# A hybrid decoder block on one core: output projection by operand, first queries ahead, norm weight per partition, table loads moved, last projection reordered, query copies on ScalarE

## The chip, the cores and the metric

The kernel runs on one core of a Trainium2 chip. A core has TensorE (matrix products, in the profile PE, its weight loads PEld), VectorE (DVE), ScalarE (ACT), GpSimd (POOL, here mostly a queue that issues transfers) and SyncE (SP, a second such queue). SBUF is the working memory of 128 partitions; PSUM holds the sums of the products. The metric is the device time of one execution in microseconds, as the median of several runs.

## The reference

One decoder block of width 1024 over 2048 positions. What is computed, cut to its frame:

```python
mod = (silu(c) @ w_ada + b_ada)                       # six vectors: sh1, sc1, g1, sh2, sc2, g2
h = rms_norm(x, norm1_g) * (1 + sc1) + sh1
gq, gk, gv, gr, glr, aq, ak, av = split(h @ w_in)     # one projection for both head groups
log_a = log_sigmoid(glr @ gla_w_gate + gla_b_gate) / 16
y_gla = gla_group(gq, gk, gv, log_a, gr, gla_norm_g)  # 4 heads of gated linear attention,
                                                      # per head rms_norm * gla_norm_g, times silu(gr)
y_att = dilated_attention_group(rms_norm(aq, q_norm_g), rms_norm(ak, k_norm_g), av)
                                                      # 8 heads, windows (128,1), (512,4), (2048,16)
x = x + g1 * (concat(y_gla, y_att) @ w_out)
h = rms_norm(x, norm2_g) * (1 + sc2) + sh2
u = causal_depthwise_conv(h @ w_up, conv_w, conv_b)   # width 3
u_gate, u_val = split(u)
x = x + g2 * ((silu(u_gate) * u_val) @ w_down)        # inner width 2816
```

All data are float32.

## The kernel before

**Tiling.** Positions are cut into four chunks of 512 (`NCH`, `T`), channels into blocks of 128. An activation tile is 128 channels by 512 positions. The large products run in three passes: an operand is split into a rounded high part and the rest, and `mm3` (L311) issues, for each block of 128 input channels, high x high (L317), high x low (L318) and low x high (L319) into one PSUM tile. Weights come through `wslot` (L243): a load into `wraw` on the POOL queue (L246), a cast to the high part on ScalarE (L251) and a difference on VectorE (L252). `plan` (L261) lists all weight blocks in the order in which the products use them, and `weights` (L300) keeps three of them ahead; `wraw` has two buffers, the parts four each.

**Stages.** Each chunk `c` goes through four:

- `proj` (L499) makes the input projection. Its operations are `q0` to `q7` (`qk`, L515: four query and four key blocks of 128 channels, that is two heads each, squares, block sums on TensorE at L526 and L527, Ln and Exp at L528 and L529, three Newton operations on VectorE at L424 to L426, the scaled result at L532, permuted copies at L536 for queries or L539 and L542 for keys), `g0` to `g3` (`glaqk`, queries and keys of the linear attention, leaving through ScalarE at L553), `W0` and `W1` (`wide`, L559: values and output gate, positions on the partitions, four PSUM tiles at once) and `V0`, `V1` (`av`, values of the attention and the low-rank gate input). The order is `ORDER0` for chunk 0 and `ORDER` for the others. `W1` holds the output gate: Tanh (L579), a copy (L580), a product (L581) and a product with `gla_norm_g`, which lies broadcast over the partitions as `gB` (L583).
- `mix` (L1067) runs `gla` (L671) for two halves of the chunk, then `attn` (L828) for four pairs of heads. `gla` prepares decayed keys and queries at several scales (L732 to L736), makes scores (L712), outputs and state (L784 to L794), takes the root of the mean square with Sqrt (L799), multiplies by the gate (L805), transposes (L811) and stores `y` through two buffers named "stage" (L814). `attn_first` (L818) loads keys and queries of the next pair of heads, the queries also into a "stage" buffer; the first pair's is called when `attn` starts (L831).
- `outproj` (L1075) loads the eight tiles of `y`, splits them (L1088, L1089), and multiplies by `w_out`: for each of eight output blocks all eight operands in turn, and the residual at L1095. The last tile, `ylast`, comes from SBUF. Then the second norm follows, and work put off to here (`self.tail`): `W1` of chunk 3 in chunk 0, the last down-projection of the chunk before in the others.
- `ffn` (L1103) makes the up-projection with convolution and gate in six groups and the down-projection (`down`, L1145).

**Order.** `run` (L1171) interleaves these as generators: `beside` and `along` (L114, L128) advance one for so many steps of another. The products of the projections of chunks 1 to 3 run beside `mix(0)`; the last five operations of the projection of chunk 3, then `outproj(0)` and `ffn(0)`, beside `mix(1)`; and so on, `outproj(3)` and `ffn(3)` alone. Over this the framework plans each engine's order with a list scheduler that has a timing model (`TC`, L38), by the order of the program as priority; each engine then runs its list strictly in order, and so do the queues of SP and POOL.

**Buffers that matter here.** PSUM has eight banks: four "psg" tiles for the large products and four "psa" for the rest. "stage" has two buffers, "pt" five. `hhi`/`hlo` have ten buffers, `ghi`/`glo` five; `y0`/`y1` two each.

**Function tables.** ScalarE holds one set of function tables. One set has Exp and Tanh, one Sqrt, one Ln and Exp together. A function outside the present set is preceded by a load (ACT_TABLE_LOAD). The set with Ln and Exp is asked for by name at the start (L339) and in `gate` (L658).

Of the kernel before, what the change touches and what calls it, by code (L numbers as in the profile page):

```python
# [32 lines left out]

ORDER0 = "g0 g1 g2 g3 V0 q0 q1 W0 q2 q3 V1 q4 q5 q6 q7 W1".split()
ORDER = "W0 V0 q0 q1 q2 g0 q3 V1 q4 g1 q5 q6 g2 q7 g3 W1".split()

# [73 lines left out]

TABS = (KD, KD, 48, 1, 1, 132, 44, 4)

# [35 lines left out]
class K:  # L148
# [49 lines left out]
    def consts(self):  # L198
        nc, A = self.nc, self.A
        self.ct = self.const.tile(list(CONSTS.shape), F32, name="consts_sb")  # L200
        self.after(nc.sync.dma_start(self.ct, A["consts"]))
        n0 = len(self.loads)
        self.mk = self.cload("masks", MASKS.shape, U32)
        self.halo = self.const.tile([P, 44, 2], F32, name="halo")

        raw = self.at.tile([P, T], F32, name="graw", tag="pt", bufs=5)
        self.gw = self.const.tile([96, 256], F32R, name="gw")
        self.tie(nc.vector.memset(raw[0:96, 0:256], 0.0), self.lastmm)
        for r in (0, 32, 64):
            self.loads.append(nc.sync.dma_start(raw[r:r + 16, 0:256], A["gla_w_gate"]))  # L210
            if r < 64:
                self.loads.append(nc.sync.dma_start(raw[r + 16:r + 17, 0:256], A["gla_b_gate"]))
        nc.vector.tensor_copy(self.gw, raw[0:96, 0:256])
        nc.vector.tensor_tensor(self.gw[32:64], raw[32:64, 0:256], self.gw[32:64].bitcast(F32), op=ALU.subtract)
        self.gB = self.cload("gla_norm_g", (P, P))
        for ld in self.loads[n0:]:
            self.after(ld)
        self.blk = self.const.tile([P, P], F32R, name="blk")
        self.tri = self.const.tile([P, P], F32R, name="tri")
        sums = self.at.tile([P, T], F32, name="sums", tag="pt", bufs=5)  # L220
        self.after(nc.sync.dma_start(sums[:, 0:2 * P], A["sums"]))
        for i, t in enumerate((self.blk, self.tri)):
            self.tie(nc.vector.tensor_copy(t, sums[:, i * P:(i + 1) * P]), self.lastmm)
        self.st = self.const.tile([P, 4, P], F32, name="state")
        nc.vector.memset(self.st, 0.0)
        self.sb = []
        for i in range(2):
            t = self.const.tile([P, 4, P], F32, name=f"sbd{i}")
            nc.vector.memset(t, 0.0)
            self.sb.append(t)  # L230
# [30 lines left out]
    def plan(self):  # L261

        def proj(c):
            for o in ORDER if c else ORDER0:
                b = int(o[1])
# [26 lines left out]
        for c in range(NCH):  # L292
            yield from (("w_out", (b,), KD, P) for b in range(KD))
            if c:
                yield from down(5)
            else:
                yield from (("w_tokw", (1, j), 2, T) for j in range(4))
            yield from ffn(c)
# [24 lines left out]
    def ada_setup(self):  # L323
# [4 lines left out]
        o = np.cumsum((0,) + TABS)  # L328
        self.n1, self.n2, self.ba, self.qg, self.kg, cw, self.cb, qsc = (tab[:, o[i]:o[i + 1]] for i in range(len(TABS)))
        self.cw = cw.rearrange("p (a b) -> p a b", a=3)  # L330
        self.qgs = self.const.tile([P, 4], F32, name="qgs")
        self.kgs = self.const.tile([P, 1], F32, name="kgs")
        self.ones = self.const.tile([P, P], F32R, name="ones")
# [4 lines left out]
        tanh = nc.scalar.activation(th, self.cond, AF.Tanh, scale=0.5)  # L338
        pre = nc.scalar.preload_act_table_set("natural_log_exp_and_others")  # L339
        self.tc.add_manual_dep(pre.ins, tanh.ins.name, mybir.DependencyInfo(mybir.DependencyClass.Sync, mybir.DependencyReason.DATA))  # L340
        nc.vector.scalar_tensor_tensor(self.cond, th, 1.0, self.cond, op0=ALU.add, op1=ALU.mult)
        nc.vector.tensor_scalar(self.qgs, qsc, self.qg[:, 0:1], -0.5, op0=ALU.mult, op1=ALU.mult)
        nc.vector.tensor_scalar(self.kgs, self.kg, -0.5, None, op0=ALU.mult)
        self.mod = self.const.tile([P, 48], F32, name="mod")
        self.G1 = self.const.tile([P, KD], F32, name="G1")
# [41 lines left out]
    def ada_late(self):  # L387
# [5 lines left out]
        for n in range(len(parts) + 2):  # L393
# [15 lines left out]
            yield  # L409


    def load_x(self, c):
# [86 lines left out]
    def proj(self, c, hs, hook=None, done=()):  # L499
# [15 lines left out]
        def qk(b):  # L515
# [19 lines left out]
            if b < 4:  # L535
                nc.vector.tensor_copy(o4.rearrange("p (r m) -> p r m", r=4), o.rearrange("p (m r) -> p r m", r=4))  # L536
                self.dq.dma_start(D["q"][b], o4)
# [21 lines left out]
        def wide(b):  # L559
# [14 lines left out]
            for s in range(4):  # L574
                off = b and put_off
                st = stage("y0" if off else None)
                if b:
                    r = stage("y1" if off else None)
                    nc.scalar.activation(st, pss[s], AF.Tanh, scale=0.5)  # L579
                    nc.scalar.copy(r, pss[s])  # L580
                    nc.vector.scalar_tensor_tensor(st, st, 1.0, r, op0=ALU.add, op1=ALU.mult)  # L581
                    heads = lambda t: t.rearrange("p (a n) -> p a n", a=4)
                    nc.vector.scalar_tensor_tensor(heads(st), heads(st), 0.5, self.gB[:, None, :].to_broadcast([P, 4, P]), op0=ALU.mult, op1=ALU.mult)  # L583
                else:
                    nc.scalar.copy(st, pss[s])  # L585
# [46 lines left out]
        ops = dict(W=wide, V=av, g=glaqk, q=qk)  # L632
        order = ORDER if c else ORDER0
        if put_off:
# [4 lines left out]
    def gate(self, c, gl):  # L639
# [12 lines left out]
        for a in range(2):  # L652
            ps = self.pa()
            for s in range(2):
                mm = nc.tensor.matmul(ps[:, s * 256:(s + 1) * 256], glr[0:96, (2 * a + s) * P:(2 * a + s + 1) * P], self.gw, start=True, stop=True)
            if a == 0:

                self.tie(nc.scalar.preload_act_table_set("natural_log_exp_and_others"), mm)  # L658
            t = self.up.tile([P, T], F32, name="gt", tag="y1")
# [10 lines left out]

    def gla(self, c, a):  # L671
        nc, D = self.nc, self.D[c]
# [105 lines left out]
        for s in range(2):  # L778
# [19 lines left out]
            yield  # L798
        nc.scalar.activation(ss, ss, AF.Sqrt, bias=self.eps, scale=1.0 / P)  # L799
        nc.vector.reciprocal(ss, ss)  # L800
        ys = []
        for s in range(2):
            y = t2("pt", 5)
            for hd in range(4):
                nc.vector.scalar_tensor_tensor(y[:, hd * P:(hd + 1) * P], os[s][:, hd * P:(hd + 1) * P], ss[:, s, hd:hd + 1], rg[s][:, hd * P:(hd + 1) * P], op0=ALU.mult, op1=ALU.mult)  # L805
            ys.append(y)
        yield
        for s in range(2):
# [3 lines left out]
            st = t2("stage", 2)  # L812
            self.copy(st, ps)
            nc.sync.dma_start(D["y"][0:4].rearrange("h p n -> p h n")[:, :, (2 * a + s) * P:(2 * a + s + 1) * P], st.rearrange("p (h n) -> p h n", h=4))  # L814
# [3 lines left out]
    def attn_first(self, c, hp):  # L818
# [3 lines left out]
        for i in range(c + 1):  # L822
            nc.sync.dma_start(kt[:, i], D[i]["k"][hp])
        qf = self.at.tile([P, T], F32, name="qf", tag="stage", bufs=2)
        nc.sync.dma_start(qf, D[c]["q"][hp])
        return kt, qf

    def attn(self, c, hp, ready):  # L828
        nc, D = self.nc, self.D
        nk = 32 * (c + 1)  # L830
        kt, qf = ready.pop() if ready else self.attn_first(c, hp)  # L831
        qn = self.at.tile([P, T], F32, name="qn", tag="pt", bufs=5)
# [233 lines left out]

    def mix(self, c):  # L1067
        for a in range(2):
            yield from self.gla(c, a)
        ready = []  # L1070
        for hp in range(4):
# [3 lines left out]
    def outproj(self, c):  # L1075
        nc, A = self.nc, self.A
        hs = []
        for k in range(KD):
            if c or k > 5:
                hi, lo = (self.hp.tile([P, T], F32R, name=n) for n in ("hhi", "hlo"))  # L1080
            elif k == 5:
                hi, lo = (self.up.tile([P, T], F32R, name=n, tag=n) for n in ("y0", "y1"))
# [8 lines left out]
        x1 = self.load_x(c)  # L1091
        for cb in range(KD):
            ps = self.pg()
            self.mm3(ps, self.weights("w_out", cb), hs)
            nc.vector.scalar_tensor_tensor(x1[cb], ps, self.mod[:, 16 + cb:17 + cb], x1[cb], op0=ALU.mult, op1=ALU.add)  # L1095
            yield
# [210 lines left out]
def layout(x, c, w_ada, b_ada, norm1_g, w_in, gla_w_gate, gla_b_gate, gla_norm_g, q_norm_g, k_norm_g, w_out, norm2_g, w_up, conv_w, conv_b, w_down):  # L1307
# [3 lines left out]
    twice = lambda a: np.concatenate([a, a])[:, None]  # L1311
    tabs = np.concatenate([colv(norm1_g[0]), colv(norm2_g[0]), colv(b_ada[0]), twice(q_norm_g[0]), twice(k_norm_g[0]), conv_w[0].reshape(3, 44, P).transpose(2, 0, 1).reshape(P, 132), colv(conv_b[0]), scale_table()], 1).astype(np.float32)
    arrs = dict(
# [7 lines left out]
        w_ch=pack_blocks(np.concatenate([w[:, 0:512], w[:, 1552:2576]], 1), P),  # L1321
        gla_w_gate=gla_w_gate[0], gla_b_gate=gla_b_gate, gla_norm_g=np.broadcast_to(gla_norm_g.reshape(1, P), (P, P)),
        w_out=pack_blocks(w_out[0], P), w_up=pack_blocks(w_up[0], P), w_down=pack_down(w_down[0]),
    )
# [17 lines left out]
```

## Time and profile before

| | us |
|---|---|
| median of three runs (2571.28 to 2572.19) | 2571.36 |
| the profiled execution | 2572.54 |
| its span, first to last instruction | 2570.7 |
| TensorE busy | 2536.8 |
| VectorE busy | 1908.6 |
| ScalarE busy | 1270.1 |
| GpSimd busy | 446.9 |
| mean granted TensorE clock, share of full | 0.997 |

A group row of the profile reads: line, engine, operation, output <- inputs, output and input shapes, count, then busy time in us and the mean of one in ns, then the idle time of the engine just ahead and what ended it. A row of a timeline reads: start in us, duration, engine, line, operation, tiles, and in brackets the idle time before it with its releaser. A row of waits reads: who waited, on whom, us in total, how often, longest. A matmul's row in the timeline is longer than its share of the engine, since matmuls overlap; the distance between two starts is what one costs.

### The profile page before, as it was taken

The numbers are of one execution on the slowest core, as the hardware profiler recorded it, in microseconds if no ns is written. First come the engines' busy times: TensorE is split into PE (matmuls) and PEld (weight loads), VectorE is DVE, ScalarE is ACT, GpSimd is POOL, SyncE is SP. The second block draws the span as 40 slices with busy tenths as digits, with TensorE's granted clock in tenths as the row PEclk, the third lists the DMA queues.
The fourth block names the chain that finished last, engine by engine and source line by source line (L and its number), as shares of the span: only waits on it lengthen the run. The fifth ranks groups of instructions, "written<-read, shape, count | busy, mean of one in ns | idle before, by whom it ended". The sixth has DMA issues, their size and how long they took to land.

```text
span 2570.7 us, 49713 instructions
## 1 busy us (share of the span) xinstructions
PE 2536.8 (99%) x19458; PEld 2092.3 (81%) x19458; DVE 1908.6 (74%) x4135; ACT 1270.1 (49%) x2624; POOL 446.9 (17%) x814
## 2 busy tenths in 40 slices
PE   7999999999999999999999999999999999999999
PEld 4888788888788888888888888888888888888887
DVE  7678877767778677777977777778777776766665
ACT  5556756655554444454545444445445443433332
POOL 2333332322310000112100000310000003200001
PEclk9999999999999999999999999999999999999999
DMA  8775675665733344446434444743444536433332
GB/s 328 265 239 188 201 251 163 222 214 162 238 120 91 115 138 141 129 158 200 140 97 131 141 141 143 232 141 107 122 141 143 149 103 209 141 97 99 98 99 82
DMA packets 189727, 406.38 MB, mean 158 GB/s; under 512 B 48515, under 2 KB 89525, under 8 KB 188213
## 3 DMA queue, kind: packets, MB, share of 16 engines
q0 software_dynamic: 88096, 308.59, 36.9%
q1 hardware_dynamic: 101396, 94.60, 12.5%
q8 instruction: 154, 2.52, 0.4%
q14 instruction: 81, 0.66, 0.1%
HBM read 341.25 MB, written 61.87 MB: 157 GB/s over the span
## 4 chain that ended last, share of the span: by engine, by line
PE 93%; DVE 2%; DMA 2%; issue 1%; ACT 1%; POOL 0%; POOLq 0%; DVEq 0%; ACTq 0%
PE psg L317 27%; PE psg L318 27%; PE psg L319 27%; PE psa L907 2%; PE psa L879 2%; PE psa L1034 2%; PE psa L712 2%; PE psa L930 1%; PE psa L1028 1%; PE psa L785 0%; PE psa L784 0%; PE psa L459 0%; PE psa L789 0%; PE psg L1212 0%; DMA y<-stage 0%
## 5 line engine op out<-in xcount | busy, mean ns | idle before, releaser
L317 PE MATMUL psg<-hhi,whi 128*128 128x512 f32 x1968 | 773.0, 394 | 0.3 <-DVE x L1163 0.3
L318 PE MATMUL psg<-hlo,whi 128*128 128x512 f32 x1968 | 770.3, 392 | 0.0
L319 PE MATMUL psg<-hhi,wlo 128*128 128x512 f32 x1968 | 770.0, 391 | 0.0
L251 ACT CAST whi<-wraw 128x1024 fp32r<-128x1024 f32 (+1 forms) x388 | 407.0, 1049 | 455.6 <-PE psg L318 392.0
L252 DVE TENSOR_TENSOR wlo<-wraw,whi 128x1024 fp32r<-128x1024 f32 (+1 forms) x388 | 474.7, 1224 | 205.7 <-ACT whi L251 198.1
L317 PEld LDWEIGHTS psg<-hhi,whi 128*128 128x128 f32 x1968 | 369.9, 188 | 78.1 <-issue 0.6
L319 PEld LDWEIGHTS psg<-hhi,wlo 128*128 128x128 f32 x1968 | 369.9, 188 | 77.2 <-issue 0.3
L318 PEld LDWEIGHTS psg<-hlo,whi 128*128 128x128 f32 x1968 | 369.9, 188 | 75.9 <-issue 0.7
L317 PE MATMUL psg<-ghi,whi 128*128 128x512 f32 x744 | 296.9, 400 | 0.3 <-DVE x L1163 0.3
L318 PE MATMUL psg<-glo,whi 128*128 128x512 f32 x744 | 293.4, 394 | 1.6 <-DVE glo L1089 1.6
L319 PE MATMUL psg<-ghi,wlo 128*128 128x512 f32 x744 | 293.0, 394 | 0.0
L246 POOL DMA_DIRECT2D wraw<-in_w_up_dram x176 | 96.8, 550 | 975.8 <-DVE wlo L252 764.1
L1163 DVE SCALAR_TENSOR_TENSOR x<-psg,mod,x 128x512 f32<-128x512 f32 x192 | 143.1, 748 | 116.2 <-PE psg L319 115.8
L317 PE MATMUL psg<-whi,hhi 128*128 128x512 f32 (+2 forms) x512 | 173.8, 344 | 2.2 <-ACT stg L585 1.5
L318 PE MATMUL psg<-wlo,hhi 128*128 128x512 f32 (+2 forms) x512 | 174.4, 342 | 0.0
L319 PE MATMUL psg<-whi,hlo 128*128 128x512 f32 (+2 forms) x512 | 173.2, 341 | 0.0
L317 PEld LDWEIGHTS psg<-ghi,whi 128*128 128x128 f32 x744 | 140.5, 189 | 31.5 <-issue 0.9
L318 PEld LDWEIGHTS psg<-glo,whi 128*128 128x128 f32 x744 | 140.4, 189 | 30.7 <-DVE glo L1089 2.3
L319 PEld LDWEIGHTS psg<-ghi,wlo 128*128 128x128 f32 x744 | 140.3, 189 | 29.6 <-issue 0.2
L1118 ACT ACTIVATE y<-psg,tables_sb 128x512 f32<-128x512 f32 x176 | 135.8, 772 | 5.4 <-PE psg L319 4.8
L1119 DVE SCALAR_TENSOR_TENSOR y<-psg,tables_sb,y 128x511 f32<-128x511 f32 x176 | 130.8, 743 | 3.5 <-ACT y L1118 3.4
L1120 DVE SCALAR_TENSOR_TENSOR y<-psg,tables_sb,y 128x510 f32<-128x510 f32 x176 | 130.6, 743 | 0.5
(279 smaller groups left out, 3610.5 us busy)
## 6 DMA issues: line engine op xcount, KB each, us to landing
wraw<-in_w_up_dram POOLq DMA_DIRECT2D x176, 512.0 KB, 3.8
wraw<-in_w_down_dram POOLq DMA_DIRECT2D x88, 512.0 KB, 3.8
wraw<-in_w_ch_dram POOLq DMA_DIRECT2D x44, 512.0 KB, 4.5
wada<-in_w_ada_dram POOLq DMA_DIRECT2D x64, 256.0 KB, 4.8
wraw<-in_w_tokw_dram POOLq DMA_DIRECT2D x32, 512.0 KB, 4.6
wraw<-in_w_out_dram POOLq DMA_DIRECT2D x32, 512.0 KB, 4.5
sq<-in_xT_dram POOLq DMA_DIRECT2D x48, 256.0 KB, 5.0
x<-x POOLq DMA_DIRECT2D x48, 256.0 KB, 5.4
```

Of the source, the lines that this page charges most:

```text
L246: ld = self.dq.dma_start(raw[:, :n], src)
L251: nc.scalar.copy(hi[:, :n], raw[:, :n])
L252: nc.vector.tensor_tensor(lo[:, :n], raw[:, :n], hi[:, :n].bitcast(F32), op=ALU.subtract)
L317: nc.tensor.matmul(ps, wh, hh, start=first and k == 0, stop=False, skip_group_check=shared)
L318: nc.tensor.matmul(ps, wh, hl, start=False, stop=False, skip_group_check=shared)
L319: self.lastmm = nc.tensor.matmul(ps, wl, hh, start=False, stop=k == n - 1, skip_group_check=shared)
L712: nc.tensor.matmul(sp[j:j + w, o + n * w:o + (n + 1) * w], kh[R, k0:k0 + w], qh[R, q0:q0 + w], start=True, stop=True)
L879: nc.tensor.matmul(at(i, hh, o, n)[H[z]], q(H[hh], i, z), key(H[hh], i, k0, n), start=True, stop=True, skip_group_check=True)
L1118: nc.scalar.activation(y, ps, AF.Identity, bias=self.cb[:, b:b + 1], scale=self.cw[:, 2, b:b + 1])
L1119: nc.vector.scalar_tensor_tensor(y[:, 1:], ps[:, :T - 1], self.cw[:, 1, b:b + 1], y[:, 1:], op0=ALU.mult, op1=ALU.add)
L1120: nc.vector.scalar_tensor_tensor(y[:, 2:], ps[:, :T - 2], self.cw[:, 0, b:b + 1], y[:, 2:], op0=ALU.mult, op1=ALU.add)
L1163: nc.vector.scalar_tensor_tensor(x1, ps, self.mod[:, 40 + cb:41 + cb], x1, op0=ALU.mult, op1=ALU.add)
```

## The change

1. `outproj`: the first four output blocks are made together, in four PSUM tiles, operand by operand: four weight blocks `w_outk`, each of two operands by 512 output channels, and within each all four outputs. The last weight block is ordered by output. Then four residual additions, and the other four output blocks as before. In chunk 0 the operands' buffers are dealt out anew: the first two operands take `hhi`/`hlo`, the next five `ghi`/`glo`, the last one `y0`/`y1`.
2. `attn_first` for the first pair of heads is called in the second `gla`, ahead of its transposes and stores; the query tile takes a "pt" buffer in place of a "stage" one.
3. `gla_norm_g` becomes a column per partition, `gy`, halved once at the start; the product at L583 and the broadcast tile go, and the evictions of the transposed outputs multiply by `gy`.
4. The set with Ln and Exp is asked for behind the Tanh at the start (as before), behind the last Tanh of each `W1` but the put-off one, and behind the Sqrt of chunk 0; no longer in `gate`.
5. The projection of chunk 3 has its own order, `ORDER3`.
6. The permuted copy of the queries (L536) moves from VectorE to ScalarE.

```diff
+ORDER3 = "W0 q0 q1 V0 q2 q3 g0 q4 q5 V1 q6 q7 g1 g2 g3 W1".split()
 ORDER = "W0 V0 q0 q1 q2 g0 q3 V1 q4 g1 q5 q6 g2 q7 g3 W1".split()
...
-            for o in ORDER if c else ORDER0:
+            for o in (ORDER0, ORDER, ORDER, ORDER3)[c]:
...
-            yield from (("w_out", (b,), KD, P) for b in range(KD))
+            yield from (("w_outk", (j,), 2, T) for j in range(4))
+            yield from (("w_out", (b,), KD, P) for b in range(4))
...
+    def logexp(self, last):
+        pre = self.nc.scalar.preload_act_table_set("natural_log_exp_and_others")
+        self.tc.add_manual_dep(pre.ins, last.ins.name, mybir.DependencyInfo(mybir.DependencyClass.Sync, mybir.DependencyReason.DATA))
...
-                nc.vector.tensor_copy(o4.rearrange("p (r m) -> p r m", r=4), o.rearrange("p (m r) -> p r m", r=4))
+                nc.scalar.copy(o4.rearrange("p (r m) -> p r m", r=4), o.rearrange("p (m r) -> p r m", r=4))
...
-                    nc.scalar.activation(st, pss[s], AF.Tanh, scale=0.5)
+                    tanh = nc.scalar.activation(st, pss[s], AF.Tanh, scale=0.5)
+                    if s == 3 and not put_off:
+                        self.logexp(tanh)
                     nc.scalar.copy(r, pss[s])
                     nc.vector.scalar_tensor_tensor(st, st, 1.0, r, op0=ALU.add, op1=ALU.mult)
-                    heads = lambda t: t.rearrange("p (a n) -> p a n", a=4)
-                    nc.vector.scalar_tensor_tensor(heads(st), heads(st), 0.5, self.gB[:, None, :].to_broadcast([P, 4, P]), op0=ALU.mult, op1=ALU.mult)
...
-            if a == 0:
-
-                self.tie(nc.scalar.preload_act_table_set("natural_log_exp_and_others"), mm)
...
-        nc.scalar.activation(ss, ss, AF.Sqrt, bias=self.eps, scale=1.0 / P)
+        root = nc.scalar.activation(ss, ss, AF.Sqrt, bias=self.eps, scale=1.0 / P)
+        if c == 0:
+            self.logexp(root)
...
+        if a:
+            ready.append(self.attn_first(c, 0))
         yield
...
-            self.copy(st, ps)
+            if s:
+                nc.scalar.activation(st, ps, AF.Copy, scale=self.gy)
+            else:
+                nc.vector.tensor_scalar(st, ps, self.gy, None, op0=ALU.mult)
...
-        qf = self.at.tile([P, T], F32, name="qf", tag="stage", bufs=2)
+        qf = self.at.tile([P, T], F32, name="qf", tag="pt", bufs=5)
...
-            if c or k > 5:
+            if c or k < 2:
                 hi, lo = (self.hp.tile([P, T], F32R, name=n) for n in ("hhi", "hlo"))
-            elif k == 5:
+            elif k == KD - 1:
                 hi, lo = (self.up.tile([P, T], F32R, name=n, tag=n) for n in ("y0", "y1"))
...
-        for cb in range(KD):
+
+        def leave(cb, ps):
+            nc.vector.scalar_tensor_tensor(x1[cb], ps, self.mod[:, 16 + cb:17 + cb], x1[cb], op0=ALU.mult, op1=ALU.add)
+
+        pss = [self.pg() for _ in range(4)]
+        for j in range(4):
+            w = self.weights("w_outk", j)
+            order = [(i, cb) for i in range(2) for cb in range(4)]
+            if j == 3:
+                order.sort(key=lambda x: x[1])
+            for i, cb in order:
+                n = slice(cb * P, (cb + 1) * P)
+                self.mm3(pss[cb], [(w[i][0][:, n], w[i][1][:, n])], hs[2 * j + i:2 * j + i + 1], i == 0 and j == 0, True)
+            if j < 3:
+                yield
+        for cb in range(4):
+            leave(cb, pss[cb])
+        yield
+        for cb in range(4, KD):
             ps = self.pg()
-            self.mm3(ps, self.weights("w_out", cb), hs)
-            nc.vector.scalar_tensor_tensor(x1[cb], ps, self.mod[:, 16 + cb:17 + cb], x1[cb], op0=ALU.mult, op1=ALU.add)
+            self.mm3(ps, self.weights("w_out", cb - 4), hs)
+            leave(cb, ps)
             yield
```

More of the change, by code (lines that the diff above doesn't have):

```diff
@@ L109 @@
 MASKS = mask_table()
-TABS = (KD, KD, 48, 1, 1, 132, 44, 4)
+TABS = (KD, KD, 48, 1, 1, 132, 44, 4, 1)
 def beside(a, na, b, nb):
@@ L214, in consts @@
         nc.vector.tensor_tensor(self.gw[32:64], raw[32:64, 0:256], self.gw[32:64].bitcast(F32), op=ALU.subtract)
-        self.gB = self.cload("gla_norm_g", (P, P))
         for ld in self.loads[n0:]:
@@ L328, in ada_setup @@
         o = np.cumsum((0,) + TABS)
-        self.n1, self.n2, self.ba, self.qg, self.kg, cw, self.cb, qsc = (tab[:, o[i]:o[i + 1]] for i in range(len(TABS)))
+        self.n1, self.n2, self.ba, self.qg, self.kg, cw, self.cb, qsc, gy = (tab[:, o[i]:o[i + 1]] for i in range(len(TABS)))
         self.cw = cw.rearrange("p (a b) -> p a b", a=3)
         self.qgs = self.const.tile([P, 4], F32, name="qgs")
-        self.kgs = self.const.tile([P, 1], F32, name="kgs")
+        self.kgs, self.gy = (self.const.tile([P, 1], F32, name=n) for n in ("kgs", "gy"))
         self.ones = self.const.tile([P, P], F32R, name="ones")
@@ L338, in ada_setup @@
         tanh = nc.scalar.activation(th, self.cond, AF.Tanh, scale=0.5)
-        pre = nc.scalar.preload_act_table_set("natural_log_exp_and_others")
-        self.tc.add_manual_dep(pre.ins, tanh.ins.name, mybir.DependencyInfo(mybir.DependencyClass.Sync, mybir.DependencyReason.DATA))
+        self.logexp(tanh)
         nc.vector.scalar_tensor_tensor(self.cond, th, 1.0, self.cond, op0=ALU.add, op1=ALU.mult)
@@ L343, in ada_setup @@
         nc.vector.tensor_scalar(self.kgs, self.kg, -0.5, None, op0=ALU.mult)
+        nc.vector.tensor_scalar(self.gy, gy, 0.5, None, op0=ALU.mult)
         self.mod = self.const.tile([P, 48], F32, name="mod")
@@ L578, in wide @@
                     r = stage("y1" if off else None)
-                    nc.scalar.activation(st, pss[s], AF.Tanh, scale=0.5)
+                    tanh = nc.scalar.activation(st, pss[s], AF.Tanh, scale=0.5)
+                    if s == 3 and not put_off:
+                        self.logexp(tanh)
                     nc.scalar.copy(r, pss[s])
                     nc.vector.scalar_tensor_tensor(st, st, 1.0, r, op0=ALU.add, op1=ALU.mult)
-                    heads = lambda t: t.rearrange("p (a n) -> p a n", a=4)
-                    nc.vector.scalar_tensor_tensor(heads(st), heads(st), 0.5, self.gB[:, None, :].to_broadcast([P, 4, P]), op0=ALU.mult, op1=ALU.mult)
                 else:
@@ L632, in proj @@
         ops = dict(W=wide, V=av, g=glaqk, q=qk)
-        order = ORDER if c else ORDER0
+        order = (ORDER0, ORDER, ORDER, ORDER3)[c]
         if put_off:
@@ L654, in gate @@
             for s in range(2):
-                mm = nc.tensor.matmul(ps[:, s * 256:(s + 1) * 256], glr[0:96, (2 * a + s) * P:(2 * a + s + 1) * P], self.gw, start=True, stop=True)
-            if a == 0:
-                self.tie(nc.scalar.preload_act_table_set("natural_log_exp_and_others"), mm)
+                nc.tensor.matmul(ps[:, s * 256:(s + 1) * 256], glr[0:96, (2 * a + s) * P:(2 * a + s + 1) * P], self.gw, start=True, stop=True)
             t = self.up.tile([P, T], F32, name="gt", tag="y1")
@@ L668, in gate, with gla @@
             self.tie(st, self.lastmm)
-    def gla(self, c, a):
+    def gla(self, c, a, ready):
         nc, D = self.nc, self.D[c]
@@ L830, in attn @@
         nk = 32 * (c + 1)
-        kt, qf = ready.pop() if ready else self.attn_first(c, hp)
+        kt, qf = ready.pop()
         qn = self.at.tile([P, T], F32, name="qn", tag="pt", bufs=5)
@@ L1067, in mix @@
     def mix(self, c):
+        ready = []
         for a in range(2):
-            yield from self.gla(c, a)
-        ready = []
+            yield from self.gla(c, a, ready)
         for hp in range(4):
@@ L1311, in layout @@
     twice = lambda a: np.concatenate([a, a])[:, None]
-    tabs = np.concatenate([colv(norm1_g[0]), colv(norm2_g[0]), colv(b_ada[0]), twice(q_norm_g[0]), twice(k_norm_g[0]), conv_w[0].reshape(3, 44, P).transpose(2, 0, 1).reshape(P, 132), colv(conv_b[0]), scale_table()], 1).astype(np.float32)
+    tabs = np.concatenate([colv(norm1_g[0]), colv(norm2_g[0]), colv(b_ada[0]), twice(q_norm_g[0]), twice(k_norm_g[0]), conv_w[0].reshape(3, 44, P).transpose(2, 0, 1).reshape(P, 132), colv(conv_b[0]), scale_table(), colv(gla_norm_g.reshape(-1))], 1).astype(np.float32)
     arrs = dict(
@@ L1321, in layout @@
         w_ch=pack_blocks(np.concatenate([w[:, 0:512], w[:, 1552:2576]], 1), P),
-        gla_w_gate=gla_w_gate[0], gla_b_gate=gla_b_gate, gla_norm_g=np.broadcast_to(gla_norm_g.reshape(1, P), (P, P)),
-        w_out=pack_blocks(w_out[0], P), w_up=pack_blocks(w_up[0], P), w_down=pack_down(w_down[0]),
+        gla_w_gate=gla_w_gate[0], gla_b_gate=gla_b_gate,
+        w_outk=wide(w_out[0][:, 0:512]), w_out=pack_blocks(w_out[0][:, 512:], P), w_up=pack_blocks(w_up[0], P), w_down=pack_down(w_down[0]),
     )
```

## The prediction

> **What bounds the kernel now.** I read the page's totals and its chain first.
>
> ```profile
> span 2570.7 us, 49713 instructions
> PE 2536.8 (99%) x19458; PEld 2092.3 (81%) x19458; DVE 1908.6 (74%) x4135; ACT 1270.1 (49%) x2624; POOL 446.9 (17%) x814
> ...
> PE 93%; DVE 2%; DMA 2%; issue 1%; ACT 1%; POOL 0%; POOLq 0%; DVEq 0%; ACTq 0%
> ```
>
> TensorE is the bound from end to end. The change neither adds nor removes a product of it: the output projection has the same 192 matmuls a chunk in another order. So relief of VectorE or ScalarE is worth nothing by itself. Only the moments count in which TensorE waits, or runs below its clock. The waits of TensorE alone (waiting line, releaser, us in total, times, longest):
>
> ```profile
> PE psa L459 <- ACT sq L1205: 14.5, 1, 14.5
> PE psa L712 <- DVE pt L736: 3.4, 1, 3.4
> PE psa L527 <- DVE sqr L521: 2.7, 1, 2.7
> PE psa L930 <- DMA qf<-q: 2.1, 1, 2.1
> PE psg L318 <- DVE glo L1089: 1.6, 1, 1.6
> PE psg L317 <- ACT stg L585: 1.5, 1, 1.5
> PE psg L317 <- ACT stg L580: 0.6, 1, 0.6
> ```
>
> The first stands at the program's start, before anything the change touches. The other six add up to 11.9 us, each happens once, and all lie between 170 and 666 us. The windows around them (us; busy time of PE, PEld, DVE, ACT, POOL; then the granted clock, DMA share and GB/s) show a second price:
>
> ```profile
> 190.00:196.00 6.00, 4.49 (x54) 3.68 (x53) 4.46 (x9) 2.99 (x6) 1.63 (x4) 1.00 0.88 319
> ...
> 300.00:304.00 4.00, 4.00 (x53) 3.25 (x42) 4.00 (x10) 2.48 (x4) 1.60 (x3) 0.57 0.38 129
> ...
> 378.50:382.00 3.50, 3.50 (x58) 3.11 (x54) 1.68 (x19) 0.70 (x3) 0.30 (x2) 0.51 0.74 219
> ...
> 658.00:662.00 4.00, 0.66 (x21) 0.32 (x22) 4.00 (x7) 3.49 (x8) 1.94 (x4) 0.98 1.09 358
> 662.00:666.00 4.00, 2.46 (x35) 1.59 (x35) 4.00 (x9) 2.52 (x5) 0.96 (x3) 0.50 1.06 327
> 666.00:672.00 6.00, 5.96 (x32) 4.38 (x33) 5.95 (x13) 3.81 (x12) 4.51 (x9) 0.50 0.95 318
> ```
>
> The clock is halved right behind each of the waits of 2.1 us and more, and not in the stretch of the 1.5 us wait. What that costs is in the timeline of TensorE: two neighbours inside such a stretch, two behind it.
>
> ```profile
> 667.06 0.63 PE L317 MATMUL psg<-ghi,whi 128*128 128x512 f32 x1
> 667.49 0.63 PE L318 MATMUL psg<-glo,whi 128*128 128x512 f32 x1
> ...
> 673.02 0.39 PE L319 MATMUL psg<-ghi,wlo 128*128 128x512 f32 x1
> 673.25 0.40 PE L317 MATMUL psg<-ghi,whi 128*128 128x512 f32 x1
> ```
>
> They start 0.43 us apart, then 0.23. So of each busy us at half clock 1 - 0.23/0.43 = 0.465 us is lost.
>
> **The change part by part.**
>
> **First queries ahead** (A, the wait of 2.1 us). The first query tile of a chunk takes a "stage" buffer, which the normalised GLA outputs leave only when they are stored; its load stands behind those stores. On the queue of SP, and the landing time of such a load:
>
> ```profile
> 367.26 2.38 SPq L814 DMA_DIRECT2D y<-stage  x2
> 375.19 1.65 SPq L825 DMA_DIRECT2D qf<-q  x2
> ...
> qf<-q SPq DMA_DIRECT2D x16, 256.0 KB, 2.7
> ```
>
> The request goes out at 375.19, when TensorE is nearly there. With a "pt" buffer, and issued ahead of the last transposes, key and query loads go out before 367.26 and land 2.7 us later, some 6 us early. Moved past them on SP are the two stores of y: one to four key loads and a query load, under 1 us each, now come first. The reader of y is the output projection, a whole attention stage later. Gain: 2.1 of wait and, at 0.51 granted over 3.5 us, 3.5 x 0.465 = 1.6 of clock: 3.7 us. Only chunk 0 shows this wait; the other chunks gain nothing.
>
> **Table loads moved** (B, the wait of 2.7 us). After a Sqrt the combined table of Ln and Exp is gone, and each Ln and each Exp loads its own until the next gate. ScalarE and then VectorE ahead of that wait:
>
> ```profile
> 287.53 1.28 ACT L461 ACT_TABLE_LOAD   x1
> ...
> 290.11 1.28 ACT L462 ACT_TABLE_LOAD   x1
> ...
> 294.63 0.62 ACT L520 CAST sqr<-sq 128x512 fp32r<-128x512 f32 x1
> ```
>
> ```profile
> 292.07 0.75 DVE L479 SCALAR_TENSOR_TENSOR sq<-sq,G,rstd 128x512 f32<-128x512 f32 x1 [2.32 <-ACT rstd L462]
> ...
> 298.14 0.68 DVE L521 TENSOR_TENSOR sqr<-sq,sqr 128x512 fp32r<-128x512 f32 x1
> ```
>
> VectorE stood idle for 2.32 us because of the two loads, and after that had work without a break up to L521, for which TensorE waits. With the combined table restored right behind the Sqrt both loads go, and L521 comes up to 2.3 us earlier. That leaves a wait of 0.4 us, of the size that cost no clock. Gain 2.3 + clock. The mean of 0.57 over 4 us is 3.4 us at half: 3.4 x 0.465 = 1.6. Together 3.9; bounds 0 (the planner puts L521 as late again) and 4.3.
>
> **Last projection reordered, and output projection operand by operand** (C, the waits of 3.4 and 1.6 us). At 658 us the last projection, the first GLA half of chunk 1 and the first output projection meet on VectorE, which is busy 4.00 of 4 us in the windows above. It releases both waits late, behind the key heads (a group of them from 640 to 676 us, first and last of six operations of 0.63 to 0.75):
>
> ```profile
> 661.18 0.68 DVE L736 TENSOR_TENSOR pt<-kt,pt 128x512 f32<-128x512 f32 x1
> ...
> 665.31 0.68 DVE L1089 TENSOR_TENSOR glo<-glo,ghi 128x512 fp32r<-128x512 f32 x1
> ```
>
> ```profile
> L424 DVE SCALAR_TENSOR_TENSOR nwt<-psa,eps,sq 128x512 f32<-128x512 f32 x3 | 2.2, 747 | 0.0
> ...
> L539 DVE COPY o<-stg 128x512 f32<-128x512 f32 x4 | 2.5, 626 | 0.1
> ```
>
> ```profile
> 663.88 0.62 ACT L1088 CAST ghi<-glo 128x512 fp32r<-128x512 f32 x1 [1.48 <-DMA glo<-y]
> ```
>
> A key head costs VectorE some 4.2 us. With g1, g2, g3 last, which leave through ScalarE alone, the last head comes two column blocks of 24 x 0.227 = 5.4 us (half the gap from 673.02 to 673.25 either way) earlier, so one head of 4.2 us, more than the 3.4 us of wait, is out of L736's way. The first output block now needs the eight operands within 5.4 us, each 0.7 us behind the last; new, a pair serves four accumulators and lasts 5.4 us, so the eighth is due 19 us after the first, and the late landing in the row above no longer shows. Loads of y and x, and the weights, keep their number and the POOL queue. Gain: 3.4 + 1.6 of waits, and the busy time at 0.50 in the two windows, 2.46 + 5.96 = 8.4, x 0.465 = 3.9: 8.9 us; below, 0.
>
> **What it adds.**
>
> ```profile
> L536 DVE COPY o<-stg x16: 599/616/661, 86.7 to 616.1; 128x512 f32<-128x512 f32 x16
> ```
>
> ```profile
> L542 ACT COPY o<-stg x16: 1074/1104/1155, 142.8 to 671.6; 128x512 f32<-128x512 f32 x16
> ...
>   DVE stg L532: 11.3, 9
> ```
>
> ```profile
> L583 DVE SCALAR_TENSOR_TENSOR stg<-stg,gla_norm_g_sb x16: 674/685/693, 178.1 to 756.1; 128x512 f32<-128x512 f32 x16
> ```
>
> ```profile
> 168.12 1.28 ACT L579 ACT_TABLE_LOAD   x1
> ```
>
> Query copies on ScalarE: 16 of 0.62 us leave VectorE, and 16 come, at the price of the nearest permuting copy there 1.10, to an engine that then stands until VectorE has made the input (11.3 us over 9 such waits of the key copies). Queued behind are weight casts and PSUM evictions. Bounds: 0, and all of 16 x (1.10 + 1.25) = 37.6; nearest are the 16 key copies of the same build, in whose stretch one wait of 2.7 us stands that ScalarE had a part in. I take 2.5.
>
> Norm weight: 16 x 0.685 = 11 us leave VectorE off the path; the scale rides on evictions that exist. It could shorten the wait of 1.5 us; I take 0, above 2.1 with its neighbour of 0.6. Tanh in chunk 1 finds the combined table and needs a load of 1.28 that it did not need; the same load at 168.12 stands before the wait of 0.6: I take 0.6, bounds 0 and 1.3. Each gate loses its own load, hidden before.
>
> Four accumulators at once leave the output projection no spare PSUM buffer at its start and its middle. The eight token-major products take all four too, and the waits of 1.5 and 0.6 are theirs: 2.1/8 x 4 chunks = 1.1; bounds 0 and 4 x 1.5 = 6.
>
> Sum: 3.7 + 3.9 + 8.9 - 2.5 - 0.6 - 1.1 = 12.3 us. The profiled execution took 2572.5 with a span of 2570.7; the runs' median is 2571.4, 1.2 below it. The gain taken from the median: **2559.1 us**.
>
> **The rivals.**
>
> Waits move, not vanish. VectorE is full from 658 to 672 and around 300, and the framework plans the whole order anew, so B and C may return behind other operations. Then A's 3.7 less half the added 4.2 is left: 1.6, 2569.8 us. For it: full VectorE. Against: the change takes 21 us of work from that engine.
>
> Slower through ScalarE: each query copy holds up a PSUM eviction in order. At the upper bound, 37.6 + 1.7 against 16.5 saved: 2594 us. It decides from (16.5 - 1.7)/16 = 0.9 us of TensorE wait a copy. Against it: 16 key copies did no such thing.
>
> All of it and nothing added, with the waits of 1.5 and 0.6 gone: 16.5 + 0.4 + 2.1 = 19 us, 2552.4.
>
> The clock does not follow from these short waits. The half-clock stretches behind A and B then stay, 1.6 each: 12.3 - 3.2 = 9.1, 2562.3 us. For it: two cases are few. Against: both begin right behind a wait. [...]
>
> **How the numbers follow.** Forecast 0.54 (its own range 2554 to 2565), waits move 0.20, ScalarE 0.09, all of it 0.11, clock 0.06. A difference of 0.2%, 5.1 us, is about what a measurement of this kernel can tell. Faster: 0.54 + 0.11 + 0.06 = 0.71; the same: 0.20; slower: 0.09. The range reaches from the case of all to the moved waits, 2552 to 2571, and leaves out ScalarE and the worse half of the moved waits.
>
> **What would show it.** Right: the waits on qf, on L521's and L736's successors and on the output projection's operands are gone, the clock reads 1.00 from 290 to 680 us, and TensorE's other waits stay under 1.5 us. A is wrong if the query load still follows the stores; B if Ln and Exp still load tables in turn near 290 us; C if VectorE still ends a wait near 660 us. The whole is wrong if TensorE shows new waits over 2 us on ScalarE evictions, or at the start of the output projections.

## The result, and the profile after

| | before | after |
|---|---|---|
| median, us | 2571.78 (2571.28 to 2574.77, 4 runs) | 2553.99 (2552.55 to 2554.95, 4 runs) |
| profiled execution, us | 2572.54 | 2554.95 |
| its span, us | 2570.7 | 2553.2 |
| mean granted TensorE clock | 0.997 | 1.000 |

The ratio is 0.9928, with a 95% interval of 0.9911 to 0.9945: faster by 17.8 us, and by more than the 12.3 forecast. The median lies inside the stated range of 2552 to 2571 us, 5.1 us below the forecast of 2559.1 and at the very edge of that case's own range of 2554 to 2565.

The totals and the chain of the changed kernel's page:

```profile
span 2553.2 us, 49701 instructions
PE 2529.3 (99%) x19458; PEld 2086.9 (82%) x19458; DVE 1891.1 (74%) x4104; ACT 1279.0 (50%) x2633; POOL 446.5 (17%) x814
...
PE 94%; DVE 2%; DMA 1%; issue 1%; ACT 1%; POOL 0%; SPq 0%; POOLq 0%; DVEq 0%; ACTq 0%
```

The number of products is the same, TensorE is still the bound. VectorE lost 17.5 us of work and ScalarE gained 8.9; neither is where the time went. TensorE's own waits (who waited, on whom, us, times, longest):

```profile
PE psa L464 <- ACT sq L1232: 14.3, 1, 14.3
PE psg L1239 <- ACT x L497: 1.3, 2, 0.9
PE psa L531 <- ACT sqr L525: 1.1, 1, 1.1
PE psg L318 <- ACT stg L587: 0.6, 1, 0.6
PE psg L319 <- DVE glo L1098: 0.6, 2, 0.4
PE psg L318 <- DVE x L1190: 0.5, 2, 0.3
```

The first two rows are the start of the program, as before. Of the waits of 3.4, 2.7, 2.1, 1.6 and 1.5 us none is left; the largest behind the start is 1.1 us, a new one, at 117 us. The windows (busy time of PE, PEld, DVE, ACT, POOL; granted clock, DMA share, GB/s) read full clock where it had been half, and so does the whole stretch from 290 to 680 us:

```profile
300.00:304.00 4.00, 4.00 (x19) 3.33 (x18) 4.00 (x8) 2.57 (x5) 1.93 (x4) 1.00 0.58 227
...
290.00:680.00 390.00, 389.35 (x3401) 324.38 (x3400) 296.68 (x740) 247.93 (x539) 120.74 (x218) 1.00 0.66 217
...
662.00:666.00 4.00, 4.00 (x108) 2.91 (x108) 4.00 (x9) 1.93 (x5) 2.49 (x5) 1.00 1.00 341
666.00:672.00 6.00, 6.00 (x87) 4.78 (x88) 4.63 (x10) 2.52 (x6) 1.61 (x3) 1.00 0.98 367
```

VectorE is still full from 300 to 304 and from 658 to 666 us, but TensorE waits for none of its results there: what counted was not the amount of its work, but which of its results came late. The SP queue shows the query load ahead of the stores of y:

```profile
349.21 0.32 SPq L834 DMA_DIRECT2D qf<-q  x1
...
358.84 0.99 SPq L823 DMA_DIRECT2D y<-stage  x2
```

The account: waits behind the start, 13.1 us before (the six of the prediction, 0.7 on L1163 and 0.5 on L1057) and 3.0 after (1.1, 0.6, 0.6, 0.5 and one of 0.2), give 10.1. The half-clock stretches of before cost 1.6 + 1.6 + 3.9 = 7.1 by the prediction's 0.465, and none is left. Together 17.2 of the 17.5 us between the two spans; the rest is less than the 2.4 us that the runs of one kernel differ.

### The profile page after: what moved, and what is told of

It reads as the page before. It is cut to its first block, busy times and chain, and to the rows that moved or that the text cites. A ratio compares the mean times of both kernels' runs of the same rounds, so it can differ in the third digit from the quotient of the medians.

```text
span 2553.2 us, 49701 instructions
## 1 busy us (share of the span) xinstructions
PE 2529.3 (99%) x19458; PEld 2086.9 (82%) x19458; DVE 1891.1 (74%) x4104; ACT 1279.0 (50%) x2633; POOL 446.5 (17%) x814
## 4 chain that ended last, share of the span: by engine, by line
PE 94%; DVE 2%; DMA 1%; issue 1%; ACT 1%; POOL 0%; SPq 0%; POOLq 0%; DVEq 0%; ACTq 0%
PE psg L318 28%; PE psg L319 27%; PE psg L320 27%; PE psa L916 2%; PE psa L888 2%; PE psa L1043 2%; PE psa L714 2%; PE psa L939 1%; PE psa L1037 1%; PE psa L787 1%; PE psa L786 1%; DMA hlo<-y 0%; PE psa L791 0%; DMA wraw<-in_w_ch_dram 0%; PE psg L1239 0%
```

## The experiments

All runs start from the changed kernel, at 2554.0 us, and their times are medians; the kernel before stood between 2571.8 and 2572.4 in all of them. Each edit also makes the framework plan the whole order anew, so a run shows the edit together with its plan.

**The first queries late again.**

```diff
-        if a:
-            ready.append(self.attn_first(c, 0))
...
-        qf = self.at.tile([P, T], F32, name="qf", tag="pt", bufs=5)
+        qf = self.at.tile([P, T], F32, name="qf", tag="stage", bufs=2)
...
-        kt, qf = ready.pop()
+        kt, qf = ready.pop() if ready else self.attn_first(c, hp)
```

> The changed kernel without the first queries ahead (query tile in a stage buffer again, loaded when attention starts). Theory of the prediction: the wait of about 2.1 us on the query load returns near 360 us, with 3.4 us of half clock behind it, 1.6 us: 2554.0 + 3.7 = 2557.7 us. Rival, the clock does not follow from a wait this short: the wait returns, the clock stays 1.00, 2556.1 us. Rival, what the change gained is the luck of a new plan, so that any other plan loses it: waits of 2 us and more at other places than this one, 2560 us and over.

2560.1 us (2558.8 to 2562.3), 6.1 more. The wait is back at its place, and the load is again behind the stores; SP queue, then the wait in the timeline of TensorE, then the window behind it:

```profile
357.61 0.95 SPq L821 DMA_DIRECT2D y<-stage  x2
365.07 4.06 SPq L832 DMA_DIRECT2D qf<-q  x2
```

```profile
370.39 0.91 PE L937 MATMUL psa<-kt,qf 64*32 64x32 f32 x64 [5.82 <-DMA qf<-q]
```

```profile
369.70:376.40 6.70, 6.01 (x87) 5.98 (x88) 1.15 (x17) 3.00 (x18) 0.00 (x0) 0.50 0.28 78
```

It is larger than the 2.1 us of before because TensorE is ready for this product 11.4 us earlier (at 364.6 instead of 375.9 us), while the data let it start only 7.7 us earlier (370.39 against 378.04). The clock followed: 0.50 over the 6.70 us of that window.

**The two halves of that edit alone:** the load issued late but into a "pt" buffer, and issued early but into a "stage" buffer.

> The changed kernel with the first queries' loads issued when attention starts, as before, but into a pt buffer. Theory of the prediction, the buffer is what held them: the load no longer waits for the stores of y, and by the SP rows of before could go out near 368 us, 2.7 us of landing, in time: 2554 us, no wait on qf. Rival, the place in the queue of SP is what counts: the load still stands behind the stores, the wait on qf returns with 2 us or more, 2557.7 to 2560.1 us.

> The changed kernel with the first queries' loads issued early, but into a stage buffer again. Theory of the prediction, by the buffer: the query tile takes one of two stage buffers, so the two stores of y must follow each other through the other one, while the load itself is early: no wait on qf, 2554 us, or at most a short wait on the transposes' evictions. Rival, the stage buffers are still held by the first half's stores, the load is late and the two outputs behind it too: a wait of 2 us and more near 360 us, 2557.7 us or more.

2554.1 us (2553.0 to 2555.7) and 2552.2 us (2550.9 to 2553.6), neither with a wait on qf. With the buffer alone the plan puts the load at 347.31, ahead of the stores at 359.23. With the place alone it goes out far earlier still, at 274.6, and only the stores get in each other's way (5.28 us on the queue in place of 0.99), which nobody waits for. SP queue of the first, then of the second:

```profile
347.31 0.32 SPq L832 DMA_DIRECT2D qf<-q  x1
...
359.23 0.99 SPq L821 DMA_DIRECT2D y<-stage  x2
```

```profile
274.61 0.33 SPq L834 DMA_DIRECT2D qf<-q  x1
...
358.15 5.28 SPq L823 DMA_DIRECT2D y<-stage  x2
```

So either half is enough, and the rivals expected of both runs were wrong. The second run's time is the lowest median of all, but by 0.07%, with ranges that overlap; that is no difference this measurement can tell.

**Table loads as before.**

```diff
-                    if s == 3 and not put_off:
-                        self.logexp(tanh)
...
-        if c == 0:
-            self.logexp(root)
...
+            if a == 0:
+                self.tie(nc.scalar.preload_act_table_set("natural_log_exp_and_others"), mm)
```

> The changed kernel with the table loads where they were (asked for in the gate, not behind Tanh and Sqrt). Theory of the prediction: Ln and Exp of the key heads and of the norm load tables in turn between 260 and 320 us, some 6 to 8 loads of 1.28 us more there, and the wait on L525 or its neighbour returns: 2.3 us and 1.6 us of clock, 2554.0 + 3.9 = 2557.9 us. Rival, VectorE's relief alone had removed that wait: the loads return, TensorE shows no wait over 1 us there, 2554 us.

2558.0 us (2556.4 to 2559.4), 4.0 more. The groups of table loads between 230 and 330 us, the wait and the window behind it:

```profile
L533 ACT ACT_TABLE_LOAD x3 | 3.8, 1283 | 0.1
L534 ACT ACT_TABLE_LOAD x3 | 3.8, 1283 | 0.1
...
L466 ACT ACT_TABLE_LOAD x1 | 1.3, 1283 | 0.0
L467 ACT ACT_TABLE_LOAD x1 | 1.3, 1283 | 0.0
```

```profile
PE psa L532 <- DVE sqr L526: 3.0, 2, 2.7
```

```profile
296.50:303.20 6.70, 6.70 (x114) 5.23 (x115) 6.70 (x14) 3.38 (x5) 1.60 (x3) 0.50 0.49 142
```

The same eight loads as before, the same 2.7 us on VectorE's L526 (L521 of before), now with 6.8 us of half clock in place of 3.4. VectorE had its other relief and it did not help: this wait came from the loads.

**Order of the last projection, output projection, and both.**

```diff
-            for o in (ORDER0, ORDER, ORDER, ORDER3)[c]:
+            for o in (ORDER0, ORDER, ORDER, ORDER)[c]:
...
-            yield from (("w_outk", (j,), 2, T) for j in range(4))
-            yield from (("w_out", (b,), KD, P) for b in range(4))
+            yield from (("w_out", (b,), KD, P) for b in range(KD))
```

The first pair of lines stands for the first run, the second, with `outproj` and its buffers as before, for the second run; the third has both.

> The changed kernel with the order of the last projection as it was; the output projection stays operand by operand. Theory of the prediction: the wait of the GLA scores on VectorE near 655 us returns, 3.4 us, and half clock for 3.4 us or more, 1.6 us and up; the wait on the operands does not: 2554.0 + 5 = 2559 us. Rival, the projection by operand alone had removed both, by taking its differences off VectorE's crowded stretch: no wait over 1 us, 2554 us.

> The changed kernel with the output projection block by block and its buffers as before; the order of the last projection stays new. Theory of the prediction: the wait on the split of a late operand near 655 us returns, 1.6 us or more since nothing stands before it, with up to 1.6 us of clock: 2554.0 + 3.2 = 2557.2 us. Rival, with the heads out of the way VectorE has the operands in time: no wait over 1 us, 2554 us. If the waits of this run and of the run with the old order add up to less than 8.9 us, either edit alone would have done most of it.

> The changed kernel with both the order of the last projection and the output projection as before. The single runs cost 2.8 us (old order) and 1.8 us (old output projection), with no half clock in either. Theory of the prediction, C is worth 8.9 us and each edit alone covers most of it: the waits of about 3.4 and 1.6 us return near 655 us with some 8 us of half clock, 2554.0 + 8.9 = 2562.9 us. Rival, the two edits are worth just their sum, since VectorE was relieved by the norm weight and the query copies too: 2554.0 + 4.6 = 2558.6 us, clock 1.00.

2556.8 us (2554.7 to 2557.3), 2555.8 (2553.4 to 2557.8), and 2561.0 (2560.7 to 2561.4), 7.0 more. The waits of the run with the old order:

```profile
PE psg L318 <- ACT stg L558: 1.5, 1, 1.5
...
PE psa L714 <- DVE pt L738: 1.2, 1, 1.2
```

Those of the run with both, and the window behind them:

```profile
PE psa L713 <- DVE pt L737: 3.4, 1, 3.4
PE psg L318 <- DVE glo L1097: 1.6, 1, 1.6
```

```profile
652.80:659.50 6.70, 5.09 (x15) 3.59 (x12) 6.70 (x13) 3.97 (x10) 3.73 (x7) 0.50 1.03 360
```

With both undone the two waits of before return to a tenth of a microsecond, with half clock behind them. With one undone the waits are 1.5 us at most and the clock stays whole (a mean of 1.0 in both profiled executions): 2.8 and 1.8 us, the second no more than the runs differ. The two edits do not add up: by these waits either one keeps the crowded stretch of VectorE from halving the clock, and what the second adds is small. The wait of 1.5 us in the first run need not be the old order's: a wait of that length on the same line stands in the run with the query copies on VectorE (below), which has the new order.

**Norm weight back on VectorE.**

```diff
+                    heads = lambda t: t.rearrange("p (a n) -> p a n", a=4)
+                    nc.vector.scalar_tensor_tensor(heads(st), heads(st), 0.5, self.gB[:, None, :].to_broadcast([P, 4, P]), op0=ALU.mult, op1=ALU.mult)
...
-            if s:
-                nc.scalar.activation(st, ps, AF.Copy, scale=self.gy)
-            else:
-                nc.vector.tensor_scalar(st, ps, self.gy, None, op0=ALU.mult)
+            self.copy(st, ps)
```

> The changed kernel with the product with the broadcast norm weight back on VectorE in every output gate (16 of 0.69 us), evictions of the transposed outputs plain. Theory of the prediction, these operations lie off the path: 2554.0 us within 1, no new wait over 1 us. Rival, they delayed the evictions of the first token-major product of chunk 1 and made the wait of 1.5 us near 192 us: it returns, 2555.5 us, clock 1.00.

2557.3 us (2555.8 to 2558.8), 3.3 more:

```profile
PE psa L532 <- ACT sqr L526: 2.3, 1, 2.3
...
PE psg L319 <- ACT stg L593: 1.2, 1, 1.2
```

The second is the wait near 192 us, from 194.7 us on now, so the rival held. The chain behind it: the eviction that TensorE waits for stands on ScalarE behind a weight cast, the cast waited for its weight load, and that load was issued when VectorE's weight difference had freed its buffer. Four of the products with the norm weight stand among VectorE's work from 179.63 to 188.85 us, three of them ahead of that difference. ScalarE, then the load on the POOL queue here and in the changed kernel:

```profile
194.32 1.10 ACT L252 CAST whi<-wraw 128x1088 fp32r<-128x1088 f32 x1 [3.20 <-DMA wraw<-in_w_av_dram]
195.32 0.58 ACT L593 COPY stg<-psg 128x512 f32<-128x512 f32 x1
```

```profile
187.87 0.53 POOL L247 DMA_DIRECT2D wraw<-in_w_av_dram  x1 [1.79 <-DVE wlo L253]
```

```profile
185.13 0.54 POOL L246 DMA_DIRECT2D wraw<-in_w_av_dram  x1 [1.64 <-DVE wlo L252]
```

The changed kernel's plan also puts its first evictions (190.94) ahead of this cast (191.88). How much of the wait is the products' and how much the plan's was not separated.

The first row, 2.3 us at 115 us, stands before any of these products runs (the first at 179.63), so they can't have made it; it is the 1.1 us wait of the changed kernel, which a new plan made longer here.

**Query copies on VectorE, twice on ScalarE, and on VectorE in chunk 0 alone.**

```diff
-                nc.scalar.copy(o4.rearrange("p (r m) -> p r m", r=4), o.rearrange("p (m r) -> p r m", r=4))
+                nc.vector.tensor_copy(o4.rearrange("p (r m) -> p r m", r=4), o.rearrange("p (m r) -> p r m", r=4))
```

> The changed kernel with the query copies on VectorE again. Theory of the prediction, on ScalarE they cost TensorE 2.5 us: without them 2551.5 us, and the wait of 1.1 us on ScalarE near 116 us goes. Rival, their move was part of VectorE's relief: waits on VectorE of over 1 us between 240 and 660 us, 2556 us or more. No difference over 1 us would say that neither holds, 2554 us.

> The changed kernel with each query copy made twice on ScalarE, 16 more of about 1.1 us. Theory of the prediction, ScalarE has room and a copy costs TensorE about 0.15 us (2.5 us over 16): 2556.5 us. Rival, ScalarE in order is close to being the bound where queries are made: each added copy shows in full on TensorE, 16 x 1.1 = 17.6 us, 2571.6 us. If nothing of it shows: 2554 us.

> The changed kernel with the query copies of chunk 0 alone back on VectorE, as a try to better it: its only wait over 1 us behind the start, on ScalarE near 116 us in chunk 0, should go. If copies on ScalarE made that wait: 2553.0 us. If the wait is one of the plan and not of the copies, or goes and another comes: 2554.0 us within 1.

2554.2 us (2553.4 to 2556.1), 2554.6 (2553.7 to 2556.4) and 2554.1 (2553.3 to 2555.8, 5 runs). Three plans, no difference. In the changed kernel the 16 copies take ScalarE 1.12 us each, and it stands 14.1 us for their inputs:

```profile
L541 ACT COPY o<-stg x16: 1093/1122/1150, 85.5 to 601.0; 128x512 f32<-128x512 f32 x16
...
  DVE stg L537: 14.1, 8
```

Yet twice as many show no wait over 0.6 us on TensorE behind the start. The wait of 1.1 us at 117 us is gone in all three, with the copies doubled too: it belongs to one plan, not to the copies. With the copies on VectorE a wait of 1.5 us on ScalarE came in its place, near 653 us:

```profile
PE psg L318 <- ACT stg L558: 1.5, 1, 1.5
```

The try to better the kernel, with the copies of chunk 0 alone, gained nothing.

**Waits put in by hand.** Copies in a row on ScalarE, started by the last product of one block, hold the first product of the next; products of the last chunk keep the program's order.

```diff
+                    if c == NCH - 1 and f >= 2:
...
+                        for i in range(1 + f % 5):
+                            step = nc.scalar.copy(self.dummy, self.dummy)
+                            if i == 0:
+                                self.tie(step, self.lastmm)
+                        self.hold = step
```

> The changed kernel with twenty waits put into the up-projection of the last chunk, where nothing runs beside it: ahead of the first product of blocks 2 to 21 TensorE waits for one to five copies in a row on ScalarE that start when its last product ends (four waits of each length, about 0.9, 1.5, 2.1, 2.7 and 3.3 us); its products are held in program order there. The waits alone: 4 x 10.5 = 42 us, 2596 us. Theory of the prediction, each wait of 2.1 us and more costs 3.4 us of half clock, 1.6 us: 12 x 1.6 = 19 us, 2615 us, none behind shorter ones. Rival, the clock is set on a fixed grid of 3.41 us by how much of one period was idle (62% and over in the drops of before, 56% in a wait of 2.3 us that cost nothing): of the waits of 2.1 and 2.7 us only those drop that lie in one period, the boundaries of half-clock stretches lie a whole number of 3.41 us apart, 2603 to 2610 us.

2648.1 us (2646.1 to 2650.2). All three sums were too low, since the twenty waits came to 65.9 us and not 42, from 2.09 to 4.69 us each. The trace has twelve half-clock stretches, each 3.41 us long, and their starts lie whole multiples of 3.41 us apart (2215.0, 2232.1 and 2249.2: five each). Two waits with what followed, from the timeline and the windows:

```profile
2497.27 0.50 PE L319 MATMUL psg<-hhi,whi 128*128 128x512 f32 x1 [2.31 <-ACT stage L1154]
```

```profile
2513.43 0.50 PE L319 MATMUL psg<-hhi,whi 128*128 128x512 f32 x1 [3.39 <-ACT stage L1154]
```

```profile
2498.40:2501.70 3.30, 3.30 (x10) 2.53 (x9) 1.43 (x3) 0.62 (x1) 0.09 (x1) 0.50 0.44 159
...
2513.40:2516.80 3.40, 3.37 (x15) 2.80 (x16) 1.71 (x4) 0.62 (x1) 0.00 (x0) 1.00 0.43 154
```

The shorter wait halved the clock, the longer did not. Laid on the grid, whose periods begin at 2494.9 and 2512.0 among others, the wait that ends at 2497.27 fills 0.68 of one period; that which ends at 2513.43 is cut into 0.57 and 0.43. So the rival held in kind, and the prediction's rule, by length alone, did not: of the sixteen waits longer than 2.1 us twelve halved the clock, and three of 2.7 us and the one of 3.39 us did not. Of the 94.1 us, 65.9 are waits and 12 x 3.41 x 0.465 = 19.0 clock; the other 9.2 were not taken apart.

## Why the prediction was right, and where it was not

- **The bound** was read rightly: TensorE's waits and its clock are all that changed, and relief of the other engines gained nothing that these two do not show.
- **A**, forecast 3.7 us: shown. In the pair of kernels 2.1 of wait and the stretch at 0.51 are gone; undone, the edit costs 6.1. The prediction took buffer and place together; either does it. That this wait cost clock, as forecast, was in part luck: it lay wholly inside one period of the grid of the last section (375.95 to 378.04 us, in a period from 375.12 to 378.53), which the forecast's rule by length does not ask.
- **B**, 3.9 us: shown, 4.0 when undone, and by the path given, the loads in turn of Ln and Exp.
- **C**, 8.9 us: shown as a whole, 7.0 when undone, with 6.8 us of half clock in place of 10.2. The prediction gave the head's 4.2 us and the operands' later due times as two causes of two waits; by the single runs either relief nearly does for both.
- **What it adds**, 4.2 us: this is the term that failed, and it makes up most of the 5.5 us missing. The query copies, 2.5, cost nothing that shows: without them on ScalarE the kernel took 0.2 more, not 2.5 less, and 16 more of them cost 0.6, less than the runs of one kernel differ. The nearest row was chosen badly: the wait in the stretch of the key copies was that of the table loads, already counted as B. The extra Tanh load, 0.6: the changed kernel has the one wait of 0.6 that there was before. The four accumulators, 1.1: around the output projections of chunks 0 and 1 TensorE's waits are 0.6 us, on operands, and 0.5 (0.7 before), in those of chunks 2 and 3 none. Without this term the sum is 16.5, and with the wait of 1.5 us of the next point 18.0, near the 17.8 measured.
- **The norm weight**, taken as 0 with 2.1 above: the wait of 1.5 us is gone with it; undone it costs 3.3, of which 1.2 is that wait and the rest partly a new plan. Operations off the path can set when a result on the path comes: VectorE's weight difference ahead of the load starts at 186.37 us with three of them before it and at 183.61 without.
- **The parts do not add up.** Undone one at a time they cost 6.1 + 4.0 + 7.0 + 3.3 + 0.2 = 20.6 us, and together they gave 17.8. New plans and overlap can both go into that; no run separates them.
- **The rivals.** Waits did move in small (the 1.1 us at 117 us) and nowhere else. ScalarE fell with the doubled copies. "All of it", 2552.4 us, came nearest, 1.6 us below the result. The clock rival fell in the form given: in the trace of before the clock fell to 0.50 behind waits this short (2.09 and 2.71 us), but with the added waits it stayed at 1.00 behind 3.39 us, so their place on a grid counted as much as their length.

## What to carry to other kernels

Where TensorE is busy for 99% of the time, list its waits one by one with the granted clock behind each: six waits of 11.9 us and the 7.1 us of clock behind them held nearly all of the gain, and 17 us less work on another engine counts for what it does to these. Undo edits singly and together: two edits on one crowded stretch cost 2.8 and 1.8 us alone and 7.0 together. A cost added off the path should be priced from a wait that it is shown to make, not from one nearby that has another cause.

## What the runs showed of the hardware that was not expected

In the traces of these runs the granted clock changed on a grid of 3.41 us, and the length of a pause alone did not decide whether it fell: 2.09 us halved it (the wait on the first queries, before), 3.39 us did not (the added waits). In the trace of before it reads 0.50 from 300.03 to 303.44, from 378.53 to 381.94 and from 661.84 to 672.08 us. The third lasted 10.24 us, three times 3.413; the second begins 78.50 us behind the first and the third 361.81 us, 23 and 106 times that. As windows, each stretch followed by 3.41 us at 1.00:

```profile
300.03:303.44 3.41, 3.41 (x47) 2.77 (x38) 3.41 (x9) 2.46 (x4) 1.60 (x3) 0.50 0.33 109
303.44:306.85 3.41, 3.41 (x16) 2.78 (x16) 3.41 (x8) 2.63 (x6) 0.39 (x1) 1.00 0.63 203
...
378.53:381.94 3.41, 3.41 (x56) 3.08 (x52) 1.62 (x17) 0.64 (x3) 0.23 (x1) 0.50 0.75 222
381.95:385.36 3.41, 3.41 (x35) 2.34 (x27) 2.26 (x12) 3.38 (x11) 1.97 (x3) 1.00 0.37 101
661.84:672.08 10.24, 8.50 (x67) 5.99 (x68) 10.19 (x22) 6.57 (x15) 5.71 (x11) 0.50 1.01 322
672.08:675.49 3.41, 3.41 (x40) 2.55 (x39) 1.91 (x4) 1.19 (x2) 2.92 (x5) 1.00 1.01 365
```

Within each of the eight executions whose waits of over 1 us behind the start were laid on that grid (before, after, and the runs with the queries late, the tables as before, the old order, order and output projection both undone, the norm weight on VectorE, and the added waits), the recorded changes of the granted clock lie whole multiples of 3.41 us apart. Counted by the idle times in the timeline's rows of these executions, a period at full clock that was idle for 0.61 and more of its length was followed by half clock (the lowest: the wait on the first queries, before, 2.09 us inside one period), and one idle for up to 0.57 was not (the highest: the 3.39 us row above). Between the two nothing was measured. The two periods as windows (TensorE busy for 1.32 of 3.41 us, then for 1.48 of 3.42):

```profile
375.12:378.53 3.41, 1.32 (x57) 1.12 (x58) 1.23 (x1) 1.04 (x1) 0.32 (x1) 1.00 0.68 197
```

```profile
2508.56:2511.98 3.42, 1.48 (x7) 0.90 (x5) 1.74 (x2) 2.59 (x4) 0.00 (x0) 1.00 0.44 153
```

Half-clock stretches lasted one period, two (6.8 us, with the queries late, the tables as before, and both undone) or three (10.2 us, before). Half-clock periods idle for 0.22 to 0.47 were followed by another one, and most of those idle for 0.16 or less were not; one idle for 0.02 was, with the tables as before, so what ends such a stretch was not settled. That one kernel would pay for a pause in one execution and not in another, depending on where it falls, is an estimate from these shares; no two traces of one kernel show it. Runs of the kernel before took from 2567.1 us, at a mean granted clock of 0.998, to 2575.9 us, at 0.996, which would fit it, but no trace of those runs shows where their clock fell. The 2.3 us at 115 us, with the norm weight on VectorE, filled at most 0.53 of a period, and the clock reads 1.00 from 113 to 122 us.
